# Ends of the gates and the combination: other places for the last raw weights, stores one product later, next weights asked for in the gates' last products, four places for the combination

## Chip, core and metric

One Trainium2 chip, one core. The metric is the device time of one execution in microseconds (us). The kernel is a whole decoder block in float32.

## What is computed

The reference, cut to the parts that the change touches (`h` is the normalised input, 2048 tokens of 1024 channels):

```python
h = _rmsnorm(x, norm_pre_mix)
proj = einsum('bsd,de->bse', h, w_in)           # q, k, v, u, z, gate_a, gate_b side by side
u, z = gelu(proj[..., U0:Z0]), gelu(proj[..., Z0:GA0])
gate_a = sigmoid(proj[..., GA0:GB0]); gate_b = sigmoid(proj[..., GB0:])
y_attn = _mixer_dilated_attention(q, k, v)      # three dilation groups, 4 heads each
                                                # alpha = softmax over the groups' log-sums
                                                # y = sum over groups of alpha * out
y_gmlp = u * (w_spatial (lower triangle) @ layernorm(z) + b)    # per chunk of 128
merged = gate_a * (y_attn @ w_branch_attn) + gate_b * (y_gmlp @ w_branch_gmlp)
y = merged @ w_out; x = x + _rmsnorm(y, norm_post_mix)
...                                             # then a squared-ReLU MLP, 1024 -> 4096 -> 1024
```

## The kernel before

A float32 product is done as three TensorE (PE) products of a high and a low part of each operand (`mm3`): the high part is a rounded copy, the low part the difference. For weights `split` makes them: the high part on POOL (L72), the low part on DVE (L78), or on POOL too for the gates. A step is three matmuls of 128x512 on one 128-row piece of the contraction; a gates product is four steps, twelve matmuls.

The tokens lie in four chunks of 512 (c = 0 to 3), two halves. The program's stages: the projections to q, k, v for all chunks (with `prenorm_cols`, which transposes normalised rows to columns, `hT`, and `keep_cols`, which stores a raw copy of them); then a long stretch in which `filler` supplies PE steps one by one (`steps(n)` takes n of them): u and z of half 1, the gates, then u and z of half 0. Between the steps stands other work: 48 attention units beside the gates, and `combine` (the softmax over the three groups) beside u of half 0. After it come merge, output projection and MLP.

PE runs in the order in which the code is written. The rows of ACT, DVE, POOL and SP are put in order by a scheduler from the dependences. Loads and stores go through SP's queue, which issues in order; it shares eight completion lanes (DMAHW0 to 7 in the rows below) with ACT's queue, and a transfer is issued when the one before it on its lane has landed.

- `keep_cols`: a copy `hr` of the transposed columns (three places, L237) is stored to `hT_d` (L238), on SP. The copy releases the transposes' bank `pt`.
- `sz_out`: the spatial product of a chunk (L545) from `z`, normalised on DVE (L573). Chunk 3's is done after step 0 of gates product t = 2.
- `gates`: 112 products t in a fixed sequence (half, operand i, column block n); the last eight (`LAST` = 104) are i = 4. Each product's raw weights are loaded four products ahead (`piece`, L613) into one of up to nine places (`raws`: 0 to 3 the first tiles, 4 and 5 the spare `ga` tiles, 6 to 8 the tiles `vs`, from which the sums of operand 5 are stored), and split on POOL three ahead (`split_piece`, into `spots`). The accumulated gates are stored to `gate_d` (L718), at the end of the product. At the last phase the columns of chunk 0 are asked for (`reload_h(0)`, `hT_b`, eight loads, L245) and u's first weights (`want(5)`).
- u of half 0 (L95 to L97, `w_u`, `hT_b`): eight products of eight steps, chunk 0 four, then chunk 1 four. `reload_h(1)` asks for chunk 1's eight loads. z's weights `w_z` come in four loads through two raw places: the third and fourth wait for DVE's low parts of the first and second.
- `combine(c)`: three loads of the groups' outputs `A` (L917), which wait for the last attention store; small operations, twelve multiplications (L937) on DVE, two additions (L939, L940; on DVE for c = 1 and 2, on POOL for c = 0 and 3); then eight transposes on PE (`yt`, L945), copies and stores. `A` has two places. The order of the chunks is 2, 3, 0, 1:

```python
    for n in range(4):
        steps((28, 18, 17, 19)[n])
        next(cs[n])
        if n < 2:
            next(cs[n + 2])
            next(cs[n + 2])
```

At the first of these calls 18 steps of the gates are still to come.

Of the kernel before, what the change touches and what calls it, by code (L numbers as in the profile page):

```python
# [8 lines left out]
F32 = mybir.dt.float32  # L9
# [7 lines left out]
P = 128  # L17
# [10 lines left out]
def f32(ap):  # L28
    return ap.bitcast(F32) if ap.dtype != F32 else ap
# [12 lines left out]
def block_kernel(ctx, tc, a, out):  # L42
    nc = tc.nc
    pe, act, dve, pool, sp = nc.tensor, nc.scalar, nc.vector, nc.gpsimd, nc.sync
# [22 lines left out]
    def split(hi, lo, src, hi_eng="act", lo_eng="dve"):  # L67

        if hi_eng == "act":
            act.activation(hi, src, AF.Copy)  # L70
        elif hi_eng == "pool":
            pool.tensor_scalar(hi, src, 1.0, 1.0, op0=OP.mult, op1=OP.mult)  # L72
        else:
            dve.tensor_copy(hi, src)
        if behind_product is not None and lo_eng == "dve":
            behind_product.append((lo, src, f32(hi)))
        else:
            (pool if lo_eng == "pool" else dve).tensor_sub(lo, src, f32(hi))  # L78
# [62 lines left out]
    gate_d = dtile([16, P, S], "gated")  # L141
# [7 lines left out]
    hT_d = dtile([4, P, KT, 512], "hTd")  # L149
# [83 lines left out]
    def keep_cols(c, i, kept):  # L233
        while kept:
            k, p3 = kept.pop(0)
            raw = xp.tile([P, 4, P], F32, name=f"hr_{c}{i}{k}", tag="hr", bufs=3)
            act.activation(raw, p3, AF.Copy)  # L237
            sp.dma_start(hT_d[c, :, k:k + 4, i * P:(i + 1) * P], raw)  # L238

    def reload_h(c):  # L240

# [339 lines left out]
    def want(q):  # L581
        if q < len(queue) and q not in loaded:
            wi, kind, n, half = queue[q]
            if kind == "z":
                loaded[q] = None if n else load_wide(wi, f"w_z{half}")
            else:
                loaded[q] = load_w(wi, f"w_{kind}{n}{half}")
# [11 lines left out]
    def piece(t):  # L599

        if t >= len(seq):
            return
        half, i, n = seq[t]
        raws = g_["raws"]
        r = raws[t % 4] if t < 8 else raws[4 + (t - LAST) % 5] if t >= LAST else raws[(t - 4) % 6]
        if i < 3:
            src = w_src(13 + n, i - 1)[:, :, :P]
        elif i == 5:
            src = s1g_d[n]
        else:  # L610
            kk, m = {6: (0, 0), 7: (0, 1), 3: (1, 0), 4: (1, 1)}[i]
            src = sg_d[n][:, kk, :, m * P:(m + 1) * P]
        sp.dma_start(r.rearrange("p (k c) -> p k c", k=4), src)  # L613
        g_["raw"][t] = r
# [35 lines left out]

    def gates():

        bank, todo = {}, []
        slots = [None, hp.tile([P, 2, 2, 4, 512], F32R, name="opB", tag="hT", bufs=2)]
        zs = wp.tile([P, 8, 512], F32, name="gz", tag="w", bufs=3)
        xs = [st.tile([P, 512], F32, name=f"gx{n}", tag="ev", bufs=3) for n in range(3)]
        g_["b"].update({(1, 1): hT[2][:, :, :4], (1, 2): hT[2][:, :, 4:]})
        phases = [(half, ops) for half in (1, 0) for ops in PHASES]
        starts, t = {}, 0
        for n, (half, ops) in enumerate(phases):  # L660
            starts[t] = n
            t += 8 * len(ops)
        for t, (half, i, n) in enumerate(seq):
            if t in starts:
                ph, t0 = starts[t], t
                if ph + 1 < len(phases):
                    s = (ph + 1) % 2
                    if not slots[s]:
                        slots[s] = hp.tile([P, 2, 2, 4, 512], F32R, name="opA", tag="hT", bufs=2)
                    for j, i2 in enumerate(phases[ph + 1][1]):  # L670
                        todo += operand(phases[ph + 1][0], i2, slots[s][:, j])
                else:
                    reload_h(0)
                    want(5)
            elif todo and (t - t0) % 3 == 1 and t > t0 + 1:
                w, k = todo.pop(0)
                with behind():
                    split(w[:, 0, k:k + 2], w[:, 1, k:k + 2], f32(w)[:, 1, k:k + 2], "act", "pool")
            piece(t + PIECES)
            split_piece(t + SPLITS)  # L680
            if i in (1, 6, 5, 4):
                bank[n] = psum_mm(f"g{half}{i}{n}")
            p, w, h = bank[n], g_["w"].pop(t), g_["b"][half, i]
            for k in range(4):
                for m, (l, r) in enumerate(((0, 0), (0, 1), (1, 0))):
                    pe.matmul(p, w[:, l, k], h[:, r, k], start=i in (1, 6, 5, 4) and not k and not m,  # L686
                              stop=k == 3 and m == 2, skip_group_check=True)
                if t == 2 and late:
                    sz_out(*late.pop(0))
                yield  # L690
            if t == 3:
                a = [ga.tile([P, 512], F32, name=f"ga{n_}", tag=f"ga{n_}", bufs=1) for n_ in range(10)]
                xs += a[:5]
                vs = a[5:8]
                g_["raws"] += a[8:] + vs
            x, z = xs[n], zs[:, n]
            if i == 1:
                act.activation(x, p, AF.Copy)
            elif i == 2:
                act.activation(z, p, AF.Copy)  # L700
                o = z, 0, 0
            elif i == 6:
                dve.tensor_add(z, x, p)
            elif i == 7:
                dve.tensor_add(x, x, p)
            elif i == 5:
                v = vs[n % 3]
                dve.tensor_add(v, x, p)
                o = v, 1, 1
            elif i == 3:  # L710
                dve.tensor_add(z, z, p)
                o = z, 0, 1
            else:
                dve.tensor_add(x, x, p)
                o = x, 1, 0
            if i in (2, 5, 3, 4):
                c = 2 * half + o[2]
                sp.dma_start(gate_d[n * 2 + o[1], :, c * 512:(c + 1) * 512], o[0])  # L718

    def filler():  # L720

# [33 lines left out]
    def steps(n):  # L755
        for _ in range(n):
            next(fill, None)
# [154 lines left out]

    def combine(c):

        A = cb.tile([P, 4, 3, 264], F32, name=f"A_{c}", tag="cA", bufs=2)
        for g in range(3):
            sp.dma_start(A[:, :, g, :], att_d[g][c * 512:(c + 1) * 512, :].rearrange("(n p) e -> p n e", p=P))  # L917
        yield
        M = sm.tile([P, 4, 4], F32, name=f"M_{c}", tag="cM")
        dve.tensor_max(M, A[:, :, 0, 260:264], A[:, :, 1, 260:264])  # L920
        dve.tensor_max(M, M, A[:, :, 2, 260:264])
        E = sm.tile([P, 4, 3, 4], F32, name=f"E_{c}", tag="cE")
        for g in range(3):
            dve.tensor_sub(E[:, :, g, :], A[:, :, g, 260:264], M)
        act.activation(E, E, AF.Exp, scale=0.125)
        Z = sm.tile([P, 4, 3, 4], F32, name=f"Z_{c}", tag="cZ")
        for g in range(3):
            dve.tensor_mul(Z[:, :, g, :], E[:, :, g, :], A[:, :, g, 256:260])
        dve.tensor_add(M, Z[:, :, 0, :], Z[:, :, 1, :])
        dve.tensor_add(M, M, Z[:, :, 2, :])  # L930
        dve.reciprocal(M, M)
        for g in range(3):
            dve.tensor_mul(E[:, :, g, :], E[:, :, g, :], M)
        for i in range(4):
            for g in range(3):
                o = A[:, i, g, 0:256].rearrange("p (j e) -> p j e", j=4)
                dve.tensor_tensor(o, o, widen(E[:, i, g, :], 64), op=OP.mult)  # L937
        eng = dve if c in (1, 2) else pool
        eng.tensor_add(A[:, :, 0, :256], A[:, :, 0, :256], A[:, :, 1, :256])  # L939
        eng.tensor_add(A[:, :, 0, :256], A[:, :, 0, :256], A[:, :, 2, :256])  # L940
        yield
        for m in range(2):
            pt = psum_aux(f"yt_{c}{m}")
            for i in range(4):
                pe.transpose(pt[:, i * P:(i + 1) * P], A[:, i, 0, m * P:(m + 1) * P], ident)  # L945
            yt = cb.tile([P, 512], F32, name=f"ya_{c}{m}", tag="cya", bufs=2)
            act.activation(yt, pt, AF.Copy)
            sp.dma_start(ya_d[m, :, c * 512:(c + 1) * 512], yt)
        yield
# [47 lines left out]
    cb = stack(ec, "cb", 2, side="right")  # L997
    cs = [combine(c) for c in (2, 3, 0, 1)]
    for n in range(2):
        next(cs[n])  # L1000
        next(cs[n])
    for n in range(4):
        steps((28, 18, 17, 19)[n])
        next(cs[n])
        if n < 2:
            next(cs[n + 2])
            next(cs[n + 2])
    ec.close()
    ega.close()

# [978 lines left out]
```

## Time and profile before

| | |
|---|---|
| median of three runs | 2695.0 us (2693.25 to 2697.19) |
| the profiled execution, own time | 2693.69 us |
| its span in the trace | 2692.0 us |
| mean granted clock of PE | 0.99 |
| busy share PE / DVE / POOL / ACT | 98 / 62 / 44 / 39% |

The span is the time from the first to the last instruction in the trace; the execution's own time is 1.7 us longer. Rows name a line of the kernel, the engine, the operation and the tiles (out<-in); the bracket behind a row of the timeline is the engine's idle time ahead of it and what ended it. `L686` is a gates matmul, `L95` to `L97` the three of a projection step.

### The profile page before, as it was taken

What the parts mean: (1) busy time and instruction counts of PE and PEld (TensorE: products, weight loads), DVE (VectorE), ACT (ScalarE), POOL (GpSimd) and SP (SyncE); (2) the same over time, 40 slices, a digit from 0 to 9 for tenths busy, and PEclk for the clock granted to TensorE, in tenths of its full rate; (3) what the DMA queues carried; (4) which work ended last, traced back from release to release, by engine and by line L of the source; (5) the groups of instructions that cost most, each with busy time, mean ns of one, the idle gap of its engine ahead of it and who ended that gap; (6) DMA issues with size and microseconds to landing.
All of it is one profiled execution on the core that took longest, in us unless ns stands there. A gap on an engine that the chain in (4) does not pass through costs nothing. (4 is left out here: it accounts for less than half of the span.)

```text
span 2692.0 us, 35404 instructions
## 1 busy us (share of the span) xinstructions
PE 2629.0 (98%) x12482; PEld 2196.3 (82%) x12482; DVE 1657.3 (62%) x2855; ACT 1061.1 (39%) x2151; POOL 1189.2 (44%) x1075
## 2 busy tenths in 40 slices
PE   9999999999999978999999999999999999999998
PEld 8888888788888866888778888888888888888887
DVE  5676674335544545665566755555437888888866
ACT  5213211154454312354445555565545333233334
POOL 0363354374555523210143464323314776676645
PEclk9999999999999998999999999999999999999999
DMA  8779878488998887554576465554343212222236
GB/s 320 277 247 332 287 234 276 136 271 250 288 280 246 231 263 249 173 195 153 184 248 239 147 204 170 183 177 129 106 145 121 87 55 87 92 85 87 89 109 212
DMA packets 379939, 515.70 MB, mean 192 GB/s; under 512 B 56497, under 2 KB 235441, under 8 KB 377970
## 3 DMA queue, kind: packets, MB, share of 16 engines
q1 hardware_dynamic: 302224, 435.51, 50.4%
q0 software_dynamic: 13360, 45.88, 4.4%
q10 hardware_dynamic: 64178, 32.06, 4.0%
q8 instruction: 98, 1.61, 0.2%
q14 instruction: 79, 0.65, 0.1%
HBM read 337.00 MB, written 176.36 MB: 191 GB/s over the span
## 5 line engine op out<-in xcount | busy, mean ns | idle before, releaser
L1840 PE MATMUL ya<-T_spots,s 128*128 128x512 f32 x1176 | 289.5, 389 | 0.7 <-ACT T_spots L70 0.6
L1840 PEld LDWEIGHTS ya<-T_spots,s 128*128 128x128 f32 x1176 | 220.6, 188 | 47.5 <-ACT T_spots L70 0.9
L70 ACT ACTIVATE s<-sraw 128x768 fp32r<-128x768 f32 (+1 forms) x184 | 127.2, 696 | 330.5 <-POOL sraw L1641 155.5
L78 DVE TENSOR_TENSOR s<-sraw,s 128x512 fp32r<-128x512 f32 x172 | 184.1, 1095 | 8.5 <-ACT s L70 8.5
L1315 PE MATMUL aa<-B,A 128*128 128x512 f32 x768 | 181.9, 389 | 0.0
L1286 POOL TENSOR_TENSOR s<-w1r 128x512 f32<-128x512 f32 x32 | 42.6, 1331 | 306.7 <-DVE S L78 262.1
L1315 PEld LDWEIGHTS aa<-B,A 128*128 128x128 f32 x768 | 143.9, 188 | 30.0 <-ACT xs L1329 0.3
L1840 PE MATMUL yc<-T_spots,s 128*128 128x512 f32 x624 | 159.7, 389 | 0.0
L686 PE MATMUL g<-opB,spots 128*128 128x512 f32 x576 | 150.7, 404 | 7.4 <-POOL spots L72 5.7
L95 PE MATMUL x<-hT_a,wq 128*128 128x512 f32 x384 | 149.7, 390 | 0.0
L96 PE MATMUL x<-hT_a,wq 128*128 128x512 f32 x384 | 149.4, 389 | 0.0
L97 PE MATMUL x<-hT_a,wq 128*128 128x512 f32 x384 | 149.4, 389 | 0.0
L686 PE MATMUL g<-opA,spots 128*128 128x512 f32 x576 | 149.0, 400 | 0.0
L1840 PEld LDWEIGHTS yc<-T_spots,s 128*128 128x128 f32 x624 | 117.1, 188 | 24.3
L686 PEld LDWEIGHTS g<-opB,spots 128*128 128x128 f32 x576 | 104.8, 192 | 28.2 <-POOL spots L72 6.3
L70 ACT ACTIVATE hl<-r 128x512 fp32r<-128x512 f32 x48 | 30.4, 633 | 234.9 <-POOL r L316 89.0
L686 PEld LDWEIGHTS g<-opA,spots 128*128 128x128 f32 x576 | 103.5, 189 | 18.0
L1640 POOL TENSOR_TENSOR sraw<-sraw 128x256 f32<-128x256 f32 x56 | 41.8, 747 | 162.0 <-DVE s L78 159.0
L78 POOL TENSOR_TENSOR T_spots<-w2r,T_spots 128x512 fp32r<-128x512 f32 x70 | 104.4, 1520 | 7.3 <-ACT T_spots L70 7.3
L909 DVE TENSOR_REDUCE o<-po 128x256 f32<-128x512 f32 x48 | 33.2, 691 | 112.9 <-PE po L908 112.9
L70 ACT ACTIVATE S<-w1r 128x512 fp32r<-128x512 f32 x96 | 60.1, 629 | 106.9 <-PE ac L1315 63.8
L72 POOL TENSOR_SCALAR spots<-gr 128x512 fp32r<-128x512 f32 x72 | 44.8, 623 | 129.0 <-PE g L686 72.0
(409 smaller groups left out, 7115.7 us busy)
## 6 DMA issues: line engine op xcount, KB each, us to landing
w1r<-in_w_mlp_in_dram SPq DMA_DIRECT2D x64, 512.0 KB, 3.8
sraw<-sd SPq DMA_DIRECT2D x128, 256.0 KB, 3.3
qk<-hl SPq DMA_DIRECT2D x24, 1024.0 KB, 5.4
qq<-qk SPq DMA_DIRECT2D x96, 256.0 KB, 5.9
w2r<-in_w_mlp_out_dram SPq DMA_DIRECT2D x16, 1024.0 KB, 6.4
sd<-u ACTq DMA_DIRECT2D x63, 256.0 KB, 3.4
g<-gated SPq DMA_DIRECT2D x58, 256.0 KB, 4.4
wq_r<-in_w_in_dram SPq DMA_DIRECT2D x24, 512.0 KB, 4.7
```

The source lines that it names most:

```text
L70: act.activation(hi, src, AF.Copy)
L72: pool.tensor_scalar(hi, src, 1.0, 1.0, op0=OP.mult, op1=OP.mult)
L78: (pool if lo_eng == "pool" else dve).tensor_sub(lo, src, f32(hi))
L95: pe.matmul(ps, lh, rh, start=start, stop=False)
L96: pe.matmul(ps, lh, rl, start=False, stop=False)
L97: pe.matmul(ps, ll, rh, start=False, stop=stop)
L686: pe.matmul(p, w[:, l, k], h[:, r, k], start=i in (1, 6, 5, 4) and not k and not m, stop=k == 3 and m == 2, skip_group_check=True)
L909: dve.tensor_reduce(ot[:, :, j * 64:(j + 1) * 64], po.rearrange("p (b h e) -> p b e h", b=4, h=2), axis=AX.X, op=OP.add)
L1286: pool.tensor_add(s1, a21, a22)
L1315: pe.matmul(p, w[:, l, k, :], h[:, r, k, :], start=i in (1, 6, 5) and not k and not n, stop=k == 3 and n == 2, skip_group_check=True)
L1640: pool.tensor_add(a22, a21, a22)
L1840: pe.matmul(p, s[:, l], w[r], start=i in (1, 2, 5) and not m and not o, stop=m == 1 and o == 2, skip_group_check=True)
```

## The change

The last eight raw weights go to a list of places of their own. A gate is stored at the end of the next product instead of its own (line L700; the last at L723). Column stores of chunks 2 and 3 are issued by ACT. Chunk 3's `sz_out` moves from product 2, step 0, to product 3, step 2. u's second weights (`want(6)`) are asked for at t = 106. `A` has four places, all twelve loads and the four combinations are written ahead of the steps, and the transposes stand after 40, 14, 14 and 14 steps.

```diff
 keep_cols
-            sp.dma_start(hT_d[c, :, k:k + 4, i * P:(i + 1) * P], raw)
+            (sp if c < 2 else act).dma_start(hT_d[c, :, k:k + 4, i * P:(i + 1) * P], raw)
 piece
-        r = raws[t % 4] if t < 8 else raws[4 + (t - LAST) % 5] if t >= LAST else raws[(t - 4) % 6]
+        r = raws[t % 4] if t < 8 else raws[(4, 5, 4, 5, 8, 6, 7, 4)[t - LAST]] if t >= LAST else raws[(t - 4) % 6]
 gates
-        bank, todo = {}, []
+        bank, todo, out_ = {}, [], []
...
+            if t == LAST + 2:
+                want(6)
             piece(t + PIECES)
...
-                if t == 2 and late:
+                if (t, k) == (3, 2) and late:
                     sz_out(*late.pop(0))
...
+            while out_:
+                sp.dma_start(*out_.pop())
             if i == 1:
...
-                sp.dma_start(gate_d[n * 2 + o[1], :, c * 512:(c + 1) * 512], o[0])
+                out_.append((gate_d[n * 2 + o[1], :, c * 512:(c + 1) * 512], o[0]))
+        sp.dma_start(*out_.pop())
 combine
-        A = cb.tile([P, 4, 3, 264], F32, name=f"A_{c}", tag="cA", bufs=2)
+        A = cb.tile([P, 4, 3, 264], F32, name=f"A_{c}", tag="cA", bufs=4)
 the main sequence
     for n in range(2):
+        for z in cs:
+            next(z)
+    for n in range(4):
+        steps((40, 14, 14, 14)[n])
         next(cs[n])
-        next(cs[n])
-    for n in range(4):
-        steps((28, 18, 17, 19)[n])
-        next(cs[n])
-        if n < 2:
-            next(cs[n + 2])
-            next(cs[n + 2])
```

Lines behind the edits shift: L686 becomes L688, the combination's L937 L942, its transposes L945 L950.

SP's rows at the gates' end, before (`ga`: the places 4 to 8; `gated`: a gate's store; `ga_4497` and `ga_4498` are places 4 and 5, `ga_4494` to `ga_4496` the places 6 to 8 from which stores go out):

```order
L613 DMA ga_4497<-sgd 128x4x128 [waits DMAHW1_49,Pool_49]
L613 DMA ga_4498<-sgd 128x4x128 [waits DMAHW2_49,Pool_49]
L718 DMA gated<-ga_4496 128x512 [waits DMAHW3_49,DVE_49]
L718 DMA gated<-gz 128x512 [waits DMAHW4_49,DVE_49]
L613 DMA ga_4496<-sgd 128x4x128 [waits DMAHW5_49,DMAHW3_49]
L783 DMA att_76<-o_8073 128x1056 [waits DMAHW6_49,DVE_49,Activation_49]
L718 DMA gated<-ga_4494 128x512 [waits DMAHW7_49,DVE_49]
L613 DMA ga_4494<-sgd 128x4x128 [waits DMAHW7_49,DMAHW0_49]
L718 DMA gated<-gz 128x512 [waits DMAHW1_49,DVE_49]
L613 DMA ga_4494<-sgd 128x4x128 [waits DMAHW2_49,DMAHW0_49,Pool_49]
L718 DMA gated<-ga_4495 128x512 [waits DVE_49]
L613 DMA ga_4495<-sgd 128x4x128 [waits DMAHW4_49,DMAHW3_49]
```

And now (places 4 and 5 are `ga_4496` and `ga_4497`, 6 to 8 `ga_4493` to `ga_4495`):

```order
L613 DMA ga_4496<-sgd 128x4x128 [waits DMAHW6_49,Pool_49]
L91 DMA w_u_r_8939<-in_w_in_dram 128x1024 [waits DMAHW7_49]
L812 DMA qq_8756<-qk_70 128x1x512 [waits DMAHW0_49,PE_49]
L812 DMA qq_8756<-qk_70 128x1x512 [waits DMAHW1_49]
L613 DMA ga_4497<-sgd 128x4x128 [waits DMAHW2_49,Pool_49]
L700 DMA gated<-ga_4495 128x512 [waits DMAHW3_49,DVE_49]
L700 DMA gated<-gz 128x512 [waits DMAHW4_49,DVE_49]
L613 DMA ga_4495<-sgd 128x4x128 [waits DMAHW5_49,DMAHW3_49]
L613 DMA ga_4496<-sgd 128x4x128 [waits DMAHW6_49,Pool_49]
L788 DMA att_76<-o_8073 128x1056 [waits DMAHW7_49,DVE_49,Activation_49]
L700 DMA gated<-ga_4493 128x512 [waits DMAHW0_49,DVE_49]
L613 DMA ga_4493<-sgd 128x4x128 [waits DMAHW1_49,DMAHW0_49]
```

The two loads that wait for POOL alone were those of products 109 and 110 and are now those of 106 and 107; the loads that also wait for a store (a second DMAHW) are now of 108 to 110. The stores stand where they stood between the loads.

SP's rows behind the combination's first loads, before (`w_z_r`: raw weights of z; `hT_b`: columns of chunk 1):

```order
L91 DMA w_z_r_9200<-in_w_in_dram 128x1024 [waits DMAHW0_49,Pool_49]
L245 DMA hT_b_9216<-hbd 128x1024 [waits DMAHW1_49,PE_49]
L245 DMA hT_b_9216<-hbd 128x1024 [waits DMAHW2_49]
L91 DMA w_z_r_9204<-in_w_in_dram 128x1024 [waits DMAHW7_49,DMAHW3_49,DVE_49]
L91 DMA w_z_r_9208<-in_w_in_dram 128x1024 [waits DMAHW4_49,DMAHW0_49,DVE_49]
L245 DMA hT_b_9216<-hbd 128x1024 [waits DMAHW5_49]
L245 DMA hT_b_9216<-hbd 128x1024 [waits DMAHW6_49]
L245 DMA hT_b_9216<-hbd 128x1024
L91 DMA w_z_r_9212<-in_w_in_dram 128x1024 [waits DMAHW3_49,DVE_49]
L245 DMA hT_b_9216<-hbd 128x1024 [waits DMAHW1_49]
L245 DMA hT_b_9216<-hbd 128x1024 [waits DMAHW2_49]
```

And now:

```order
L91 DMA w_z_r_9272<-in_w_in_dram 128x1024 [waits DMAHW6_49,Pool_49]
L91 DMA w_z_r_9276<-in_w_in_dram 128x1024 [waits DMAHW7_49,Pool_49]
L245 DMA hT_b_9288<-hbd 128x1024 [waits DMAHW0_49,PE_49]
L245 DMA hT_b_9288<-hbd 128x1024 [waits DMAHW1_49]
L91 DMA w_z_r_9280<-in_w_in_dram 128x1024 [waits DMAHW6_49,DMAHW2_49,DVE_49]
L91 DMA w_z_r_9284<-in_w_in_dram 128x1024 [waits DMAHW7_49,DMAHW3_49,DVE_49]
L245 DMA hT_b_9288<-hbd 128x1024 [waits DMAHW4_49]
L245 DMA hT_b_9288<-hbd 128x1024 [waits DMAHW5_49]
L245 DMA hT_b_9288<-hbd 128x1024 x2
L245 DMA hT_b_9288<-hbd 128x1024 [waits DMAHW0_49]
L245 DMA hT_b_9288<-hbd 128x1024 [waits DMAHW1_49]
```

Six of the eight column loads stood behind two weight loads that wait for DVE, the last three behind a third; now all six stand behind two.

DVE's rows before the second `w_z` low part, before (L937: chunk 3's multiplications, `A_9083`):

```order
L78 TENSOR_TENSOR w_z_0_9198<-w_z_r_9200,w_z_0_9198 128x4x256 [waits DMAHW0_49,Pool_49]
L931 RECIPROCAL M_9087<-M_9087 128x16 [waits DVE_49]
L933 TENSOR_TENSOR E_9090<-E_9090,M_9087 128x4x4 [waits DVE_49]
L933 TENSOR_TENSOR E_9090<-E_9090,M_9087 128x4x4 x2
L937 TENSOR_TENSOR A_9083<-A_9083,E_9090 128x256 [waits DVE_49] x3
L937 TENSOR_TENSOR A_9083<-A_9083,E_9090 128x256 x9
L78 TENSOR_TENSOR w_z_0_9198<-w_z_r_9204,w_z_0_9198 128x4x256 [waits DMAHW3_49,Pool_49]
L920 TENSOR_TENSOR M_9280<-A_9276 128x16 [waits DMAHW7_49,DMAHW0_49]
```

And now (L942: `A_9059` is chunk 3, `A_9063` chunk 0, `A_9067` chunk 1):

```order
L942 TENSOR_TENSOR A_9059<-A_9059,E_9106 128x256 [waits DVE_49] x3
L942 TENSOR_TENSOR A_9059<-A_9059,E_9106 128x256 x9
L936 RECIPROCAL M_9135<-M_9135 128x16
L925 TENSOR_TENSOR M_9167<-A_9067 128x16 [waits DMAHW1_49,DMAHW0_49]
L938 TENSOR_TENSOR E_9138<-E_9138,M_9135 128x4x4 [waits DVE_49]
L938 TENSOR_TENSOR E_9138<-E_9138,M_9135 128x4x4 x2
L942 TENSOR_TENSOR A_9063<-A_9063,E_9138 128x256 [waits DVE_49] x3
L942 TENSOR_TENSOR A_9063<-A_9063,E_9138 128x256 x9
L926 TENSOR_TENSOR M_9167<-M_9167,A_9067 128x16 [waits DMAHW2_49]
L78 TENSOR_TENSOR w_z_0_9270<-w_z_r_9272,w_z_0_9270 128x4x256 [waits DMAHW6_49,Pool_49]
```

The low part for the first `w_z` load stood ahead of chunk 3's multiplications, the second right behind them; now both stand behind those of chunk 3 and of chunk 0.

## Prediction

> **What bounds the kernel now.** The page's head first:
>
> ```profile
> span 2692.0 us, 35404 instructions
> PE 2629.0 (98%) x12482; PEld 2196.3 (82%) x12482; DVE 1657.3 (62%) x2855; ACT 1061.1 (39%) x2151; POOL 1189.2 (44%) x1075
> ```
>
> TensorE (PE) is busy for 98% of the span and the edits take no matmul away. So they can only win or lose what PE waits, plus what its clock loses behind a wait. The waits of PE, by releaser (total, times, longest), those that the edits touch:
>
> ```profile
> PE yt L945 <- POOL A L940: 11.4, 2, 10.8
> PE yt L945 <- issue: 8.8, 1, 8.8
> PE g L686 <- POOL spots L72: 5.7, 2, 3.3
> PE pt L218 <- ACT hr L237: 4.4, 1, 4.4
> PE sz L545 <- DVE z L573: 3.2, 3, 2.1
> PE sz L545 <- DVE sb L552: 1.9, 1, 1.9
> PE g L686 <- POOL spots L78: 1.0, 2, 0.6
> PE g L686 <- DVE gx L714: 0.7, 1, 0.7
> ```
>
> Four places: the column transposes (4.4 us), the late `sz` (3.2), the last gates products (5.7 + 1.0 + 0.7 = 7.4), the combination's transposes `yt` (11.4 + 8.8). A wait costs more than itself, since the clock behind it is low; stretches behind the `sz` waits and behind the 8.8 (us, PE busy, granted clock, DMA share, GB/s):
>
> ```profile
> 531.00:533.00 2.00, 1.52 (x7) 0.53 1.00 396
> 1012.00:1014.00 2.00, 2.00 (x7) 0.50 0.37 141
> ```
>
> About 5 us at half clock lose some 2.5 us more, so the 4.4 is worth up to 7.2 (estimated); the `sz` stretch loses 2.1 beside its 3.2, estimated from some 4 us at 0.5 to 0.6. The Trainium skill ("TensorE: Matmul & The Clock Gate", Part 1) says that the clock halves after an idle window of about 3.4 us; by it the `sz` waits, the longest 2.1 us, would bring no slow clock and that term would be 3.2. The trace differs (0.53 behind it), and I go by the trace.
>
> **Column stores on ACT's queue.** ACT's rows at the 4.4 us wait, and what these stores take on SP's queue in this stretch (KB, median us from issue to landing), beside a store of that size on ACT's queue:
>
> ```profile
> 225.05 1.09 ACT L237 ACTIVATE hr<-pt 128x512 f32<-128x512 f32 x2 [4.70 <-DMA hTd<-hr]
> hTd<-hr SPq DMA_DIRECT2D x8, 256.0 KB, 5.0
> sd<-u ACTq DMA_DIRECT2D x63, 256.0 KB, 3.4
> ```
>
> `hr` has three places; the fourth copy waits until the first store has landed, and SP issues that store late, behind a 1 MB store and a weight load. ACT issues it right behind the copy, some 3 us sooner. If it then takes 3.4, nearly all of the wait goes; the next copies come one store apart, so I leave 1.5 us standing. The 16 issues on ACT itself lie beside idle time (39% busy). Gain 4.5 (bounds 1.3, if it still queues behind SP's bytes, and 7.2). The Trainium skill ("DMA: Bandwidth & Descriptors", Issuing engines are not separate DMA queues) speaks against more: all issuers end on the same 16 engines and interleave, so only issue time is saved. By that rule alone the term is between 1.3 and 3.
>
> The same edit moves DVE's order: the normalise of the next columns (L113, L207) comes to stand behind L352 of `vb` and L433, L434.
>
> ```profile
> 261.67 1.29 DVE L207 SCALAR_TENSOR_TENSOR x<-x,r_pre,gpre 128x1024 f32<-128x1024 f32 x1
> 263.49 0.42 DVE L352 TENSOR_TENSOR vt<-vb,vt 128x256 fp32r<-128x256 f32 x1 [0.53 <-ACT vt L351]
> 265.63 1.04 PE L218 MATMUL pt<-ident,x 128*128 128x128 f32 x8
> ```
>
> L352 at 263.49, three operations of 0.42 and one of 0.15, then 1.29: `x` is ready at 266.2, and PE wants it at 265.63. Three blocks so, 0.6 us each plus clock: loss 2.3 (0 to 4.5).
>
> **`sz` moved.** It goes from the first step of product 2 to the third of product 3: 18 matmuls later, 18 x 0.227 = 4.1 us (a full-clock matmul of 512 columns starts every 0.227 us: 48 of them lie between 983.66 and 994.65 in the rows further down).
>
> ```profile
> 531.48 1.89 PE L545 MATMUL sz<-wsp,z 128*128 128x128 f32 x7 [0.91 <-DVE z L573]
> ```
>
> The last `z` came just ahead of 531.48. Without the 3.2 of waits PE would have been there at 528.3, and 4.1 later it is there at 532.4, behind that `z`: the 3.2 and the 2.1 of clock go, 5.2 together. What is late next is the bank of the third group (L552, 1.9 once elsewhere): lower bound 1.3.
>
> **Stores a product later, places of the last raw weights.** The rows of the gates' end:
>
> ```profile
> 964.45 0.95 PE L686 MATMUL g<-opB,spots 128*128 128x512 f32 x3
> 967.72 0.97 PE L686 MATMUL g<-opB,spots 128*128 128x512 f32 x2 [2.32 <-POOL spots L72]
> 972.58 1.05 PE L902 MATMUL pv<-pf,v 128*128 128x128 f32 x8
> 983.66 1.63 PE L686 MATMUL g<-opB,spots 128*128 128x512 f32 x6 [0.75 <-DVE gx L714]
> 994.65 0.39 PE L95 MATMUL u<-hT_b,w_u 128*128 128x512 f32 x1
> SPq L613 <- DMA gated<-ga: 14.4, 3, 6.0
> ```
>
> From 965.1 (964.45 and three issues) to 983.66 PE does two products (24 x 0.227 = 5.45) and 12 transposes and small matmuls (1.15, from the row of eight): 6.6 us of work in 18.5, so 11.9 are lost, 7.4 as waits. The last row is the cause: three loads of raw weights stand 14.4 us on SP until a store out of the same place has landed, and the splits on POOL behind them. In the new order the loads of products 106 and 107 take places 4 and 5, free since the splits of 104 and 105, and are issued where 109 and 110 were; only 108 to 110 wait for stores, two to four products (5 to 11 us) ahead of their use. So the 11.9 go and the products end at 982.8. The stores themselves hardly move in SP's row order: 0.
>
> **Weights and the four places: what comes next.** `w_u` of n=1 and all twelve loads of `A` now stand ahead of the stall point, and the transposes come after 22, 36, 50, 64 steps of `u` instead of 10, 28, 45, 64. Before:
>
> ```profile
> 1010.44 1.94 PE L945 MATMUL yt<-ident,A 128*128 128x128 f32 x8 [8.83 <-issue]
> 1026.85 1.09 PE L945 MATMUL yt<-ident,A 128*128 128x128 f32 x8 [0.53 <-POOL A L940]
> 1050.38 1.97 PE L945 MATMUL yt<-ident,A 128*128 128x128 f32 x8 [10.85 <-POOL A L940]
> 1001.70 0.18 DVE L921 TENSOR_TENSOR M<-M,A 128x16 f32<-128x16 f32 x1 [1.32 <-DMA A<-att]
> 1003.83 4.11 DVE L937 TENSOR_TENSOR A<-A,E 128x256 f32<-128x256 f32 x12
> 981.00:984.00 3.00, 2.25 (x10) 0.88 1.03 415
> ```
>
> Chunk 2: from the third `A` load (1001.6) to the transposes (1010.4) lie 8.8 us of DVE's work. That load lands behind the last attention store; eight `hT_b`, two `w_u`, some stores (some 6.6 MB) go ahead, from about 971 at up to 415 GB/s, so the store lands near 989 and the load near 996 (it was 1001.6). Ready at 1004.7 (an estimate, good to 2 us); PE arrives at 982.8 + 22 x 0.682 = 997.8: wait 6.9 against 8.83, gain 1.9, the slow clock behind it (2.6) stays. Chunk 3 (0.53 + 0.3) and chunk 0 (10.85 + 1.5) wait no more: 13.1.
>
> Now the price. Two loads of `w_z` wait for DVE's low parts of the two before (their raw places), and six of the eight loads of the next `hT_b` stand behind them on SP. DVE does these low parts behind the combination of chunks 3 and 0, POOL does their high parts behind its additions. Rows that size it:
>
> ```profile
> SPq L91 <- DVE w_z L78: 4.7, 1, 4.7
> 1014.32 1.22 DVE L78 TENSOR_TENSOR w_z<-w_z_r,w_z 128x1024 fp32r<-128x1024 f32 x1
> 1045.72 2.19 DVE L920 TENSOR_TENSOR M<-A 128x16 f32<-128x16 f32 x1
> 1020.70 3.64 POOL L939 TENSOR_TENSOR A<-A 128x1024 f32<-128x1024 f32 x1 [3.37 <-DVE A L937]
> 1024.42 2.38 POOL L940 TENSOR_TENSOR A<-A 128x1024 f32<-128x1024 f32 x1
> 1045.54 2.34 POOL L939 TENSOR_TENSOR A<-A 128x1024 f32<-128x1024 f32 x1 [18.74 <-DMA ud<-ut]
> 1010.66 1.05 POOL L72 TENSOR_SCALAR w_u<-w_u_r 128x1024 fp32r<-128x1024 f32 x1 [13.92 <-DMA w_u_r<-in_w_in_dram]
> hT_b<-hbd SPq DMA_DIRECT2D x8, 512.0 KB, 7.0
> ```
>
> From 1004.7: small operations of both chunks 3.7, chunk 3's twelve multiplications 4.1 (1012.5); POOL's two additions 4.7 and chunk 0's multiplications 4.1; a high part 1.05, a low part 1.22; POOL's addition for chunk 0 2.34, a high part 1.05, a low part 1.22. The row at 1045.72 is a DVE operation of 0.17 us that took 2.19 while POOL added: the two shut each other out. Then all these add up, to 1028.2, with one addition of 3.64 to 1029.5; I take 1030 for the last `w_z` load's release. Side by side it would be 1023; with every addition slow, 1034. From there the fourth `hT_b` load lands 7 us on, the others 1.26 apart (512 KB at 415 GB/s); so the last two at 12 us, and the product of `u`, which reads them pair by pair, ends two steps (1.4) behind: 13.4 on, at 1043.4. Unstalled PE would end it at 1021.4 (1004.7, transposes 1.9, 18 steps 12.3, some slow clock 1.4, the next transposes 1.1). So PE stalls 22, with a us of clock 23 (16 to 27), where before the same queue cost nothing.
>
> Gates and combination: 11.9 + 1.9 + 13.1 - 23 = **+4** (0 to 11).
>
> **Sum.** 4.5 - 2.3 + 5.2 + 4 = 11.4 us of gain. The profiled run took 2693.69 (span 2692.0), 1.3 under the median: 2693.7 - 11.4 = 2682.3, as a median 2683.6. With all terms at their ends together the gain is between -2 and 23.5: 2671.5 to 2697.
>
> **Rivals.** (A) *The next `hT_b` is in time*: DVE and POOL work side by side and PE, held up elsewhere, doesn't reach these steps first. For it: before, the same loads waited 4.7 us and PE lost nothing. Against: then only one chunk stood ahead of the low parts, now two. The stall of 23 goes: gain 34.4, median 2660.6. Chance 0.14. (B) *Slower*: DVE's multiplications starve beside POOL. One took three times the usual:
>
> ```profile
> L937 DVE TENSOR_TENSOR A<-A,E x36: 410/418/1261, 1003.8 to 1045.2; 128x256 f32<-128x256 f32 x36
> ```
>
> If all 24 of chunks 3 and 0 took 1.26 instead of 0.42, the release comes 20 us later, at 1050, the stall is 43 and the whole change loses 8.6: 2703.6. It decides from about 1047, where the loss passes 5.4 us (0.2%, what a measurement of this kernel tells from no change). Against: only POOL's four additions stand there, 9.4 to 12 us. Chance 0.14. (C) *No change*: the ACT store lands behind SP's bytes (1.3), L207 costs 4.5, `sz` meets its bank (1.3), the stall is 27 (0): -1.9, about 2697. It does what the words say, at no profit. With neighbours within 5.4 us, 0.14.
>
> **How the numbers follow.** My forecast has 0.58, nearly all of it beyond 0.2%. Faster: 0.56 + 0.14 = 0.70; same 0.15 (C and a little of the forecast's edge); slower 0.15. The likeliest case's own range is 2672 to 2692; the range leaves out the middle of A and B: 2664 to 2696.
>
> **What would show it.** Right: no wait of `g` on `spots` behind product 105, gates ending about 12 us sooner against the transposes; `yt` waiting once, 5 to 9 us; and a stall of 15 to 27 us, in pieces, at `u` (L95) on DMA `hT_b`, between that wait and the second `yt`, with SP held on DVE `w_z`. Wrong: no `u` wait on `hT_b` (then A), or one over 40 (B); `pt` still waiting 4 us on `hr`; `sz` waiting 3 us.

## The result and the profile after

The changed kernel takes 2700.48 us (median of 20 runs, 2692.37 to 2705.62) where the kernel before takes 2694.7 (20 runs): a ratio of 1.0019, 95% interval 1.0010 to 1.0027. It is slower by 0.1 to 0.3%; the forecast was 11 us faster. The profiled execution took 2699.51 us, its span is 2697.8.

The head of the page and the waits of PE, by releaser (total, times, longest), that answer to those shown of before:

```profile
span 2697.8 us, 35401 instructions
PE 2628.7 (97%) x12482; PEld 2192.5 (81%) x12482; DVE 1664.2 (62%) x2855; ACT 1058.4 (39%) x2149; POOL 1186.9 (44%) x1075
...
PE u L95 <- DMA hT_b<-hbd: 15.3, 2, 14.0
PE g L688 <- POOL spots L72: 10.5, 1, 10.5
PE pt L218 <- DVE x L207: 5.1, 5, 2.5
PE yt L950 <- issue: 4.6, 1, 4.6
PE u L95 <- DVE ga L718: 3.1, 1, 3.1
PE pt L218 <- ACT hr L237: 3.1, 1, 3.1
PE u L96 <- DMA hT_b<-hbd: 2.3, 2, 1.6
```

The `yt` waits of 20.2 us have shrunk to 4.6, the waits of `sz` on `z` are gone. In their place stand 17.6 us of `u` on the columns `hT_b`, which the prediction had, and 10.5 us of a gates product on its weights, which it had not. The timeline says where:

```profile
224.03 1.12 PE L218 MATMUL pt<-ident,x 128*128 128x128 f32 x4 [3.09 <-ACT hr L237]
265.54 1.09 PE L218 MATMUL pt<-ident,x 128*128 128x128 f32 x8 [2.51 <-DVE x L207]
532.13 3.89 PE L545 MATMUL sz<-wsp,z 128*128 128x128 f32 x32
559.11 3.43 PE L688 MATMUL g<-hT_a,spots 128*128 128x512 f32 x6 [10.51 <-POOL spots L72]
997.04 0.50 PE L95 MATMUL u<-hT_b,w_u 128*128 128x512 f32 x1 [3.14 <-DVE ga L718]
1013.04 1.94 PE L950 MATMUL yt<-ident,A 128*128 128x128 f32 x8 [4.59 <-issue]
1041.48 0.80 PE L95 MATMUL u<-hT_b,w_u 128*128 128x512 f32 x1 [13.96 <-DMA hT_b<-hbd]
```

The bracket at 559.11 does not stand at the gates' end but at the ninth of 112 products, 27 us behind the moved `sz`. Both traces hold 12482 matmuls of PE, and their order differs only at `sz` and at the combination's transposes; so elsewhere each can be set against its counterpart. The difference after minus before, at places between the events:

```
place (us, before)                    after - before (us)   what lies between
219, ahead of the wait for hr          -0.4                  no edit
262, column transposes                 -2.8                  ACT's stores: -2.4
300, behind the column transposes      +0.9                  x late: +3.6
545, behind sz                         -4.4                  sz moved: -5.3
562, eleventh gates product            +9.0                  wait at 559 and its slow clock: +13.4
956, last attention units              +5.3                  a wait for kp of 3.4 is now 0.5: -3.7
984, gates' end                        -6.3                  raw places: -11.7
1000, u under way                      -3.0                  u waits for DVE: +3.3
1060, behind the combination           +2.9                  yt's waits against hT_b's: +6.0
end of the span                        +5.8                  merge and MLP: +2.9
```

The first expectation below gives the wait at 559 as 12.8: that is the difference at 555, where the clock is still slow (0.51 granted from 555 to 565 in the changed kernel).

### The profile page after: what moved, and what is told of

It reads as the page before. It is cut to its first block, busy times and chain, and to the rows that moved or that the text cites. A ratio compares the mean times of both kernels' runs of the same rounds, so it can differ in the third digit from the quotient of the medians.

```text
span 2697.8 us, 35401 instructions
## 1 busy us (share of the span) xinstructions
PE 2628.7 (97%) x12482; PEld 2192.5 (81%) x12482; DVE 1664.2 (62%) x2855; ACT 1058.4 (39%) x2149; POOL 1186.9 (44%) x1075
## 5 line engine op out<-in xcount | busy, mean ns | idle before, releaser
L688 PE MATMUL g<-opA,spots 128*128 128x512 f32 x576 | 148.4, 399 | 0.0
L688 PE MATMUL g<-opB,spots 128*128 128x512 f32 x576 | 147.0, 398 | 0.0
L688 PEld LDWEIGHTS g<-opB,spots 128*128 128x128 f32 x576 | 103.5, 188 | 18.5
L688 PEld LDWEIGHTS g<-opA,spots 128*128 128x128 f32 x576 | 103.1, 189 | 18.0
L78 DVE TENSOR_TENSOR A<-w1r,A 128x512 fp32r<-128x512 f32 x61 | 62.1, 1018 | 70.8 <-ACT A L70 70.8
```

## The experiments

Each time stands beside the median of the kernel before that was measured with it (2694.6, 2691.0 or 2689.7 us). Where these medians differ, compare the ratios and not the times. The expectations speak of POOL's additions for `sz`; in the code they are multiplications (L555).

**What makes the wait at 559.** Two suspects among the edits: the moved `sz` and the stores a product later.

*sz back.* Edit, on the changed kernel:

```diff
-                if (t, k) == (3, 2) and late:
+                if t == 2 and late:
```

> The changed kernel with only sz_out of chunk 3 put back to product 2, step 0. Theory Q (the moved sz takes its stores, loads and POOL additions past the raw weights' loads on SP and POOL, and this makes the wait of 10.5 us for spots at 559): that wait goes, the sz waits of about 3 us at 529 return with some 2 us of slow clock; 12.8 - 5.3 = 7.5 us less than the changed kernel, about 2693. Rival S (the gates' stores one product later hold up SP there): the wait stays at 8 us or more and the sz waits come on top, 5 us more than the changed kernel.

2691.17 us against 2694.57, ratio 0.9987 (0.9977 to 0.9998). Its trace has no wait of a gates product near 559; `sz` waits again, the last of four brackets (0.90, 0.85, 0.27 and 0.60 us):

```profile
535.50 5.74 PE L545 MATMUL sz<-wsp,z 128*128 128x128 f32 x26 [0.60 <-DVE z L573]
```

As theory Q had it: by the two ratios some 9 us less than the changed kernel.

*Stores back in their own product.* Edit, on the changed kernel: the list `out_` goes and the store stands where it stood.

```diff
-            while out_:
-                sp.dma_start(*out_.pop())
...
-                out_.append((gate_d[n * 2 + o[1], :, c * 512:(c + 1) * 512], o[0]))
+                sp.dma_start(gate_d[n * 2 + o[1], :, c * 512:(c + 1) * 512], o[0])
```

> The changed kernel with each gate's store put back to its own product, all else as changed. Theory Q: the wait at 559 stays at 9 to 12 us, and the time is the changed kernel's within 3 us. Rival S: the wait falls below 3 us and the time by 10 or more.

2701.51 us, ratio 1.0022 (1.0012 to 1.0032), within the changed kernel's interval, and the wait is 11.12 us. The stores' place is worth nothing that these runs can tell, here as at the gates' end.

*The stores of sz's result on POOL's queue.*

```diff
-            sp.dma_start(yg_d[g, :, c * 512:(c + 1) * 512], t)
+            (pool if c == 3 else sp).dma_start(yg_d[g, :, c * 512:(c + 1) * 512], t)
```

> The changed kernel with the four stores of chunk 3's sz result issued by POOL instead of SP; the sums themselves stay where they are. If SP is held by waiting for POOL's additions (four stores, 10.4 us of waits), the wait for spots falls to 3 us or less and the time by 8 to 12 us. If it is POOL's own order (the additions between the splits), it stays at 7 us or more.

```profile
561.05 4.29 PE L688 MATMUL g<-hT_a,spots 128*128 128x512 f32 x8 [10.69 <-POOL spots L72]
```

2697.18 us, ratio 1.0008 (0.9998 to 1.0019), the wait unmoved. So it is not that SP is held by these four stores. But the second reading that I had offered, POOL's multiplications between the splits, doesn't follow either. In the changed kernel SP, and POOL's idle time, show a third:

```profile
552.36 2.30 SPq L613 DMA_DIRECT2D gr<-sgd  x2
554.75 1.01 SPq L613 DMA_DIRECT2D ga<-in_w_in_dram  x2
...
558.44 0.62 POOL L72 TENSOR_SCALAR spots<-ga 128x512 fp32r<-128x512 f32 x1 [4.18 <-DMA ga<-in_w_in_dram]
```

The weights of products 8 and 9 (places 4 and 5, `ga`) are asked for at 554.75, when PE has stood without them for 6 us. Before, this was done at 545.08 and 546.13:

```profile
545.08 0.45 SPq L613 DMA_DIRECT2D ga<-in_w_in_dram  x1
546.13 0.42 SPq L613 DMA_DIRECT2D ga<-in_w_in_dram  x1
```

In the row order these two loads stood behind five loads of later products, one of which is a phase ahead (`gr<-sgd`); now they stand behind eight, four of them a phase ahead, each waiting for a split on POOL. The reason is in the code: `ga`'s tiles are made from the memory of the pool that holds `z` (`ez.close()`, then `stack(ega, "ga", 1)`), so these loads wait for `sz`'s last matmul, and a later `sz` made the scheduler put them later. With `sz` back (above) SP issues both at 549.66, again behind one load of the later phase only.

*Products 8 to 11 in the first four places.* With `sz` still moved:

```diff
-        r = raws[t % 4] if t < 8 else ...
+        r = raws[t % 4] if t < 12 else ...
```

> The changed kernel, sz_out at its new place, but the raw weights of products 8 to 11 in the four first places instead of 8 and 9 in the two ga places. Theory M (those two places lie in the memory that z holds until sz has read it; with a later sz the scheduler puts these two loads behind eight later ones, four of which wait for POOL): products 8 and 9 get their weights in time, the wait of 10.5 us near 559 falls to 3 us or less, the time by 8 to 12 us. Rival P (POOL's additions for sz between the splits make the splits late, wherever the loads stand): the wait stays at 6 us or more.

2689.54 us against 2690.99, ratio 0.9992 (0.9981 to 1.0003), by the ratios some 7 us less than the changed kernel: the wait for weights is gone, but half of its length, 5.54 us, comes back as a wait for ACT. PE, ACT and DVE of this run, in the order of the chain:

```profile
560.91 1.62 PE L688 MATMUL g<-hT_a,spots 128*128 128x512 f32 x3 [5.54 <-ACT ga L702]
...
557.02 1.28 ACT L868 ACT_TABLE_LOAD   x1 [10.15 <-DVE nm L865]
...
547.13 0.75 DVE L552 SCALAR_TENSOR_TENSOR sb<-sz,lngb,bsp 128x512 f32<-128x512 f32 x1 [11.64 <-POOL spots L78]
548.24 0.75 DVE L552 SCALAR_TENSOR_TENSOR sb<-sz,lngb,bsp 128x512 f32<-128x512 f32 x1 [0.37 <-DMA ygd<-sb]
554.87 0.29 DVE L862 CUSTOM_DVE_ANT_0 e<-s,mask 128x128 f32<-128x128 f32 x1 [5.88 <-DMA ygd<-sb]
```

Read it from the bottom: the first attention unit's `e` waits for a store of `sz`'s result to land, since its pool too is opened on `z`'s memory (`ez.close()`, then `stack(e1b, "at", ...)`). The exponentials wait for it on ACT, and the copies that empty the gates' banks stand behind them on ACT. Theory M holds for half of the wait; the other half is the same late release by a second way. Not all of that half need be the moved `sz`: in the changed kernel `e` started at 551.54, 3.3 us sooner than here. In this run POOL does the first of `sz`'s multiplications late, behind two splits whose load came late:

```profile
538.73 0.62 POOL L72 TENSOR_SCALAR spots<-gr 128x512 fp32r<-128x512 f32 x1 [6.26 <-DMA gr<-in_w_in_dram]
...
542.63 1.28 POOL L555 TENSOR_TENSOR sb<-sb,ur 128x512 f32<-128x512 f32 x1
```

There it was done at 540.04. How much of the 5.54 us this order cost was not measured. Theory P is refuted for the first half: the multiplications stood between the splits, and no product waited for a split.

**What the combination gains and gives back.** In the changed kernel, on SP and DVE:

```profile
SPq L91 <- DVE w_z L78: 14.8, 2, 10.9
...
1032.37 4.75 SPq L91 DMA_DIRECT2D w_z_r<-in_w_in_dram  x2
1037.17 2.93 SPq L245 DMA_DIRECT2D hT_b<-hbd  x6
...
1019.42 2.21 DVE L925 TENSOR_TENSOR M<-A 128x16 f32<-128x16 f32 x1
1021.55 2.54 DVE L938 TENSOR_TENSOR E<-E,M 128x16 f32<-128x16 f32 x3
1024.02 4.94 DVE L942 TENSOR_TENSOR A<-A,E 128x256 f32<-128x256 f32 x12
1031.13 1.21 DVE L78 TENSOR_TENSOR w_z<-w_z_r,w_z 128x1024 fp32r<-128x1024 f32 x1
1035.55 1.21 DVE L78 TENSOR_TENSOR w_z<-w_z_r,w_z 128x1024 fp32r<-128x1024 f32 x1
```

*Columns ahead of z's weights.* On the changed kernel `reload_h(1)` moves ahead of `want(q + 2)`:

```diff
+            if (kind, n, half) == ("u", 0, 0):
+                reload_h(1)
             if (kind, n) == ("u", 1) or (kind, n, half) == ("u", 0, 0):
                 want(q + 2)
...
-                if not half and (ci, n) == (0, 0):
-                    reload_h(1)
```

> The changed kernel with chunk 1's column loads asked for ahead of z's weights (one statement moved), so that no column load stands behind a weight load that waits for DVE. Theory: the u waits on hT_b (1.3 + 0.7 + 14.0 + 1.6 = 17.6 us) go, with the slow clock behind them some 20 us; the time falls by 15 to 20 us, to 2680 to 2686. Rival: the time is owed to the combination itself and turns up again at the second or third yt or at the first z product: the fall is below 6 us.

2683.13 us against 2694.57, ratio 0.9955 (0.9943 to 0.9967): 17 us less than the changed kernel. The waits for columns are 3.1 us together, nothing of the gain comes back but 1.7 us at a later `yt`. So 17 of the 22 us that the stall cost hung on one row order on SP.

*The raw places alone*, on the kernel before (the one line of `piece`).

> The kernel before with only the list of places for the last eight raw weights. Theory (the places end the gates' waits, but the combination's first transposes hang on the attention store and the A loads, not on PE): the waits of g on spots at the gates' end go (11.6 us by the changed kernel), the first yt waits 13 to 16 us instead of 8.8, and the gain is 4 to 7 us. Rival: the gates' gain comes through whole: 10 to 12 us.

```profile
1002.59 1.94 PE L945 MATMUL yt<-ident,A 128*128 128x128 f32 x8 [14.56 <-DVE M L921]
```

2688.3 us against 2690.99, ratio 0.9983 (0.9974 to 0.9992): 4.6 us by the ratio, as in theory. The gates' waits go; ahead of the combination PE is 13.5 us ahead of before, behind this `yt` 7.8. Measured at the transposes, nearly half of the gates' gain was a loan: it was paid back at the next thing that hung on a DMA, the attention store and the loads of `A`.

**ACT's stores**, alone on the kernel before:

```diff
-            sp.dma_start(hT_d[c, :, k:k + 4, i * P:(i + 1) * P], raw)
+            (sp if c < 2 else act).dma_start(hT_d[c, :, k:k + 4, i * P:(i + 1) * P], raw)
```

> The kernel before with only the stores of chunks 2 and 3's columns on ACT's queue. Theory: the first store lands as late as on SP's queue, behind the bytes that SP has asked for (some 7 us), so pt still waits 2 to 4 us on hr, and x (L207) comes 2 to 4 us too late once at about 265: between 1 us faster and 2 us slower. Rival, the prediction's: 2 to 5 us faster.

2693.9 us, ratio 1.0009 (0.9999 to 1.0020): 2.4 us lost by the ratio, with an interval from nothing to 5.4. The rival's gain is excluded; the theory's range, up to 2 us slower, is not. In this run's trace the wait for `hr` is 2.16 us and PE gains 4.6 us by it, counted as in the table above; then `x` takes 7.9 us back:

```profile
265.80 1.54 PE L218 MATMUL pt<-ident,x 128*128 128x128 f32 x6 [3.68 <-DVE x L207]
```

In the changed kernel's trace, the store on ACT's queue in this stretch (KB, median us to landing), its first issue and the copy that waits for it; last, the first issues of before, on SP:

```profile
hTd<-hr ACTq DMA_DIRECT2D x6, 256.0 KB, 5.4
...
215.94 0.42 ACTq L238 DMA_DIRECT2D hTd<-hr  x1
223.38 0.60 ACT L237 ACTIVATE hr<-pt 128x512 f32<-128x512 f32 x1 [4.52 <-DMA hTd<-hr]
...
219.76 1.84 SPq L238 DMA_DIRECT2D hTd<-hr  x3
```

The first store is issued 3.8 us sooner, but the copy that it releases starts only 1.7 us sooner (223.38 against 225.05).

**Put together.** The changed kernel with three repairs: products 8 to 11 in the first places, columns first, and ACT's queue for chunk 2 alone (`act if c == 2 else sp`), which leaves DVE's order in chunk 3 as it was.

> The changed kernel with products 8 to 11 in the first places, chunk 1's column loads ahead of z's weights, and ACT's queue for chunk 2's column stores alone. If the three losses are separate they add up: the wait near 559 (10 to 12 us), the u waits on hT_b (17 us) and the wait for x at 265 (2.5 to 3.6 us) go: 2668 to 2674. If one gain is given back at the next wait (the first yt, the first z product), 2676 or more.

2670.31 us against 2690.99, ratio 0.9913 (0.9899 to 0.9926): faster than both kernels, by 20.7 and, set against the ratio of the changed kernel, some 28 us. The losses add up nearly whole, though 5.7 us of the wait near 559 are left, on ACT. With DVE's order as it was, ACT's queue does pay by the traces: counted from 219 to 300, PE gains 2.3 us on the kernel before here, and 1.9 and 2.0 in the next two runs.

*The same with `sz` back at product 2* and the `ga` places for products 8 and 9:

> The changed kernel with sz_out of chunk 3 back at product 2, chunk 1's column loads ahead of z's weights, ACT's queue for chunk 2's columns alone (products 8 and 9 in the ga places, as changed). Theory (the moved sz is worth its 5 us only while the memory of z, reused for raw weights and for the attention units, is not wanted; the delay of its release costs at least as much): the wait of 5.7 us near 558 that the version before still had goes, 2 to 3 us of sz waits return: equal to it or up to 4 us faster, 2666 to 2671. Rival (the moved sz is a net gain once the places are mended): 3 to 6 us slower, 2673 to 2676.

2669.01 us against 2689.69, ratio 0.9912 (0.9896 to 0.9927): no difference that can be told, with intervals of some 4 us to either side. The move of `sz` is worth nothing that these runs can tell, even with the places mended; its cost to the attention units was not mended in the version beside it.

*Transposes after 48, 10, 12 and 12 steps*, on the version with three repairs:

```diff
-        steps((40, 14, 14, 14)[n])
+        steps((48, 10, 12, 12)[n])
```

> The version with products 8 to 11 in the first places, columns first and ACT's queue for chunk 2's columns, with the transposes after 48, 10, 12, 12 steps instead of 40, 14, 14, 14. Theory: the first yt, 5.9 us late there, is the only late one of the four by more than 3 us, and eight steps of 0.682 = 5.5 us more ahead of it cover it: 5 to 8 us faster with its slow clock, 2662 to 2666. Rival: the chunks behind it come late instead (POOL's additions for chunks 3 and 0), and what the first wait loses stands at the second or third: within 3 us of 2670.

```profile
999.86 1.06 PE L950 MATMUL yt<-ident,A 128*128 128x128 f32 x8 [0.37 <-issue]
1009.01 0.77 PE L95 MATMUL u<-hT_b,w_u 128*128 128x512 f32 x1 [6.70 <-DMA hT_b<-hbd]
```

2668.62 us, ratio 0.9924 (0.9912 to 0.9936) beside 0.9913: the rival's outcome, though not by its way. The first `yt` waits no more; PE comes to chunk 1's columns 8 us sooner (at 1002.3 against 1010.5) and waits 6.7 there. By SP's rows of this run, what stands behind the first transposes now is the pace of SP's queue, which issues `A`, gates and columns one behind another:

```profile
978.85 18.55 SPq L922 DMA_DIRECT2D A<-att  x12
997.50 2.30 SPq L700 DMA_DIRECT2D gated<-ga  x2
999.89 0.41 SPq L723 DMA_DIRECT2D gated<-ga  x1
1000.40 7.87 SPq L245 DMA_DIRECT2D hT_b<-hbd  x8
```

No run tested that by another order.

## Why the prediction was wrong, point by point

- **The term that failed is `sz` moved** (5.2 us of gain, "what is late next is the bank of the third group"). The gain was there (5.3), but I followed the step on PE alone. It issues loads, sums and stores on SP, DVE and POOL, and its `z` lies in memory that raw weights and attention tiles get next. Its later end moved two loads behind eight others and held DVE: +13.4 us, so the term came out as a loss of 8.1. The new order of SP's rows showed both loads at their new places ahead of the run; I had read that order at the ends of the gates and not at the start. The run with `sz` back shows it for the whole, the run with other places for half.
- **ACT's stores** (4.5 gain, 2.3 loss) failed too: in the profiled execution they cost 1.3 us (2.4 of gain, 3.6 of loss) in place of the 2.2 gained by forecast. In the six other runs that hold the whole edit the gain is 2.7 to 5.0, the loss 4.3 to 8.2 and the sum 1.5 to 4.5 us lost: it is the lateness of `x` that was mis-sized most. Nearly all of it came at the first of three places (2.8 of 3.6 us). On the gain, I took 3.4 us to landing from a later stage, the MLP; here the DMA engines are full (a share of 1.03 to 1.14 from 214 to 230), the store took 5.4 in the median, and the copy still waited 4.52. The rule of the Trainium skill that spoke against the term ("DMA: Bandwidth & Descriptors", Issuing engines are not separate DMA queues) left 1.3 to 3: the changed kernel's trace agrees with 2.4, the run with this edit alone, with 4.6, does not.
- **The raw places** were right: 11.9 forecast, 11.7 measured. The stores a product later were right at nothing at the gates' end; the `kp` wait that shrank by 2.9 (3.7 with its slow clock) was not in the sum, and as it is between nothing and 2.0 us in the other runs, with late stores and without, no edit can be named for it.
- **The combination** was right in mechanism and nearly in size. The stall stood where it was forecast; the second low part ends 24 us behind chunk 2's, forecast 25.3; the loss is 17.6 us of waits and 22 with its slow clock, forecast 23. DVE's one small operation of 0.17 us took 2.21 beside POOL's addition (1019.10 to 1021.59), so they added up as in the likeliest case. Not forecast: 3.1 us of `u` on DVE at 997.04. DVE stood idle for 14 us ahead of a low part of `w_u`, whose high part waited for its load, with the last gates' sums, which empty PE's banks, behind it:

```profile
995.16 1.22 DVE L78 TENSOR_TENSOR w_u<-w_u_r,w_u 128x1024 fp32r<-128x1024 f32 x1 [14.14 <-POOL w_u L72]
996.31 0.68 DVE L718 TENSOR_TENSOR ga<-ga,g 128x512 f32<-128x512 f32 x1
```

- **Gates and combination together**: +4 forecast, 2.4 measured (from +5.3 at 956 to +2.9 at 1060).
- **Rivals.** The time came near the slower rival's side, by none of its means, so that nearness is luck: one multiplication took 1.25 us, as one did before, and the twelve 4.94. The error of 17.2 us is made up of 13.3 for `sz`, 3.5 for ACT, 1.6 for gates and combination and 2.9 in merge and MLP, where no edit lies; 3.7 at `kp` and 0.4 ahead of all edits go the other way. In merge and MLP the other runs stand between 1.9 us below and 3.4 above before; what makes it is left open.

## What to carry to other kernels

A step that is moved ends its tiles later, too: ask what memory it frees, and look in the built order for every load that takes that memory, wherever in the program it stands. A wait that is removed ahead of a chain hung on DMAs comes back at the chain; the gain is what the next late transfer leaves of it (7.8 of 13.5 us here). And a load that must wait for a slow engine should not stand ahead, in an in-order queue, of loads that wait for nothing: one moved statement was worth 17 us.

## What the runs showed of the hardware that was not expected

A 256 KB store issued right behind its copy on ACT's queue took 5.4 us from issue to landing (median of 6), no less than the 5.0 (median of 8) of the same stores on SP's queue before, while the DMA engines were full. The first was issued 3.8 us sooner and released its copy 1.7 us sooner: a second queue with little in it brought the issue forward, but less than half of that came through at the landing. The rows that say how full, from the changed kernel (us, PE busy, clock, DMA share, GB/s):

```profile
214.00:218.00 4.00, 4.00 (x22) 1.00 1.03 371
218.00:222.00 4.00, 2.94 (x15) 1.00 1.14 346
```
